# The first layer's modulation of a two-block kernel, computed by GpSimd instead of TensorE

## The chip, the cores and the metric

The kernel runs on one core of a Trainium2 chip. The metric is device time in microseconds, the median of several executions. The engines that matter are TensorE (PE in the tables, its weight loads PEld), VectorE (DVE), ScalarE (ACT), GpSimd (POOL) and SyncE (SP), which issues most loads.

## What is computed

A first block of two layers (a causal mixer, cross-attention to a memory, a gated feed-forward) works on 256 tokens of 1024 features. A second block of two layers (pooling, gating and neighbourhood attention, then a feed-forward) follows; its norms and residuals are modulated by a condition vector. The part that the change touches is this modulation, for layer 0 of the second block:

```python
silu_c  = jax.nn.silu(c)        # 1024 values, for the latents
silu_cc = jax.nn.silu(c_ctx)    # 1024 values, for the context
mod   = silu_c  @ w_mod[l] + b_mod[l]     # w_mod[l] is 1024 x 6144 float32
mod_c = silu_cc @ w_mod[l] + b_mod[l]
sh1, sc1, g1, sh2, sc2, g2 = jnp.split(mod[:, None, :], 6, axis=-1)
a = rms_norm_2(h, norm1_g[l]) * (1 + sc1) + sh1     # and so on
```

So it is a product of two rows of 1024 with a matrix of 25 MB, which depends on no activation: it can be done at any time before the second block begins.

## The kernel before

Activations are held by features: 128 partitions, eight feature tiles, 256 tokens. Every weight piece (512 KB mostly) is loaded by `pieces` through SyncE's queue into `raw` (three buffers), split by `split` into two float32r parts, `hi` by ScalarE (line 254) and `lo = raw - hi` by VectorE (line 255), four buffers each, and multiplied three times by TensorE (`mm3`, lines 226 to 228). A unit of a feed-forward of the first block (`swiglu`) takes six such pieces, and VectorE also makes the gated hidden values there (lines 779 to 783: `g` and `a` from PSUM, then `g`, `a` and the split of `a` in SBUF).

`modulation_0` is a generator of 48 steps. A step loads a 512 KB piece of `w_mod0` (four row tiles of 256 columns) through GpSimd's queue into `fraw` (three buffers), and TensorE multiplies its four row tiles by four windows of `cs`, a tile in which the two condition columns stand between columns of zeros, each on its own 32 columns of the array (line 140, a bank of PSUM `fmm`). So twelve groups of columns gather in one bank, each on its own rows. After 24 steps ScalarE copies the bank (`modrow`, line 144), two products with the selector `sel` (line 147) turn it to features and add the four quarters, and VectorE adds the bias into `modT` (line 149). The steps are placed by `tick`, which issues them behind an instruction of TensorE's (token sums, scores), and what is left is done by `modulation_done(0)` in the hook `context` of the second feed-forward. The second layer's `modulation_1` works on VectorE, later, and isn't touched.

The order of each engine's queue is made by a scheduler at build time from the program's order and its own estimates of time; on the chip each engine works through its queue in that order. An engine that waits holds up all that is queued behind.

Of the kernel before, what the change touches and what calls it, by code (L numbers as in the profile page):

```python
# [22 lines left out]
# Column offsets of the per-feature vectors (feature k * 128 + p lies at [p, offset + k]).  # L23
VEC = {}
# [16 lines left out]
def _spec():  # L41
    """How each weight matrix is cut: groups of columns in the order of use, each a list of pieces
    (first row tile, row tiles, columns) of at most 4 KB a partition."""
# [24 lines left out]
    s["w_mod0"] = cut(8, 6 * D, 256, 4)  # L68
# [30 lines left out]
class Block:  # L99
    """Weights of one stream piece, split into float32r parts whose sum they are."""  # L100
# [6 lines left out]
def kernel(ctx: ExitStack, tc: tile.TileContext, A: dict, out: bass.AP):  # L107
# [7 lines left out]
    def enter(name, side="left", **bufs):  # L115
        """Opens a pool for the temporaries with these tags (and numbers of buffers)."""
# [11 lines left out]
    def modulation_0():  # L128
        """shift, scale and gate of the first layer's streams, by features: steps of four products, for where the tensor
        engine waits. Twelve groups of 256 features share a bank, each on its rows; a quarter of the array adds up a  # L130
        quarter of the sum over the features of the condition."""
        for c in range(24):
            j = c % 12
            for off, k0, kt, n in OFFSETS["w_mod0"][c]:
                if j == 0 and k0 == 0:
                    ps = bank("fmm")
                w = temp("fraw", [128, kt, n])
                load(w.rearrange("p k n -> p (k n)"), "w_mod0", off, nc.gpsimd)
                for k in range(4):
                    nc.tensor.matmul(ps[32 * k:32 * k + 32, :256], cs[:, k0 + k, 22 - 2 * j:54 - 2 * j], w[:, k, :],  # L140
                                     start=j == 0 and k0 == 0, stop=j == 11 and k0 == 4, tile_position=(0, 32 * k))
                if j == 11 and k0 == 4:
                    m = temp("modrow", [128, 256])
                    nc.scalar.activation(m, ps[:, :256], AF.Copy)
                    ps = bank("fmm")
                    for i in range(2):
                        nc.tensor.matmul(ps[:, 32 * i:32 * i + 24], m[:, i * 128:i * 128 + 128], sel, start=True, stop=True)
                    o = VEC["b_mod_2"][0] + 2 * c - 22
                    nc.vector.tensor_tensor(modT[:, 0, 2 * c - 22:2 * c + 2, :].rearrange("p (c i) s -> p i c s", i=2),
                                            ps[:, :64].rearrange("p (i c s) -> p i c s", i=2, s=2)[:, :, :12, :],  # L150
                                            vecs[:, o:o + 24].rearrange("p (c i) -> p i c", i=2)[:, :, :, None]
                                            .to_broadcast([128, 2, 12, 2]), op=OP.add)
                yield True
# [1241 lines left out]
```

## Time and profile before

| | |
|---|---|
| median of three runs | 1993.68 us (1992.7 to 1998.14) |
| span of the profiled execution | 1991.1 us |
| PE, PEld busy | 1944.0, 1762.3 us (98%, 89%) |
| DVE, ACT, POOL busy | 1350.4, 864.3, 85.0 us |
| loads of `w_mod0` (`fraw`) | 48 of 512 KB, from GpSimd's queue |

The profiled execution's span lies 2.6 us under the median. The stages, by the first loads of their weights: the first mixer to about 135 us, its output and the first cross-attention to 200, the first feed-forward to about 390, the second layer of the first block to 590, its feed-forward to about 800, the second block from there to the end. Busy shares of an engine are averages; what is worth reading is, stage by stage, which engine has no idle time left and what it waited for. The rows have a section of their own below.

### The profile page before, as it was taken

Reading aid. Unit: us, or ns where it says so; the run is one execution under the profiler, and the core shown is the slowest. Engines: PE = TensorE matmul, PEld = TensorE weight load, DVE = VectorE, ACT = ScalarE, POOL = GpSimd, SP = SyncE. Lnnn points to the kernel's source line nnn. Section 1 sums busy time; section 2 is a strip of 40 time slices with the busy share of each in tenths; the row PEclk is TensorE's granted clock in tenths of the full one; section 3 lists DMA queues with packets and bytes.
Section 4 is the critical chain, followed back from the end, with each engine's and each line's share of the span. In section 5 each row is a group of like instructions: output and inputs, shape, how many; then the busy total and the mean of one; then the engine's idle time right before and its main releaser. Section 6 shows DMA issues by size and latency. Waiting matters only on the chain.

```text
span 1991.1 us, 34583 instructions
## 1 busy us (share of the span) xinstructions
PE 1944.0 (98%) x13852; PEld 1762.3 (89%) x13852; DVE 1350.4 (68%) x2790; ACT 864.3 (43%) x1477; POOL 85.0 (4%) x163
## 2 busy tenths in 40 slices
PE   7999999999999999999999999999999899999998
PEld 6689999998889999798788888888889898989998
DVE  7567766686686767645677765777775755667666
ACT  6565544445564444434432233333223434444444
POOL 1100000000000000000011100111100000000000
PEclk9999999999999999999999999999999999999999
DMA  7656555653356555322256532444432432554553
GB/s 262 238 182 223 180 184 182 195 184 115 120 197 223 197 180 180 100 86 67 72 163 182 164 106 85 140 151 150 151 122 86 158 106 85 185 186 142 188 184 112
DMA packets 89776, 309.43 MB, mean 155 GB/s; under 512 B 10528, under 2 KB 15552, under 8 KB 89360
## 3 DMA queue, kind: packets, MB, share of 16 engines
q1 hardware_dynamic: 74048, 254.43, 39.1%
q0 software_dynamic: 15280, 52.28, 8.1%
q8 instruction: 108, 1.77, 0.4%
q14 instruction: 52, 0.43, 0.1%
q10 hardware_dynamic: 288, 0.52, 0.1%
HBM read 306.15 MB, written 1.05 MB: 154 GB/s over the span
## 4 chain that ended last, share of the span: by engine, by line
PE 93%; issue 2%; DVE 2%; DMA 1%; ACT 1%; POOL 0%; DVEq 0%; POOLq 0%; ACTq 0%
PE mm L226 20%; PE mm L227 20%; PE mm L228 20%; PE sc L226 5%; PE sc L227 4%; PE sc L228 4%; PE pv L227 3%; PE pv L226 3%; PE pv L228 3%; PE pv L436 2%; PE sc L400 2%; PE pv L419 2%; DMA fraw<-in_w_mod 1%; PE fmm L140 1%; PE sc L358 1%
## 5 line engine op out<-in xcount | busy, mean ns | idle before, releaser
L254 ACT ACTIVATE hi<-raw 128x1024 fp32r<-128x1024 f32 (+2 forms) x466 | 487.8, 1053 | 774.0 <-PE mm L227 326.9
L255 DVE TENSOR_TENSOR lo<-raw,hi 128x1024 fp32r<-128x1024 f32 (+2 forms) x466 | 566.3, 1217 | 333.3 <-ACT hi L254 329.2
L226 PE MATMUL mm<-oph,hi 128*128 128x256 f32 (+1 forms) x1832 | 566.6, 311 | 4.2 <-ACT oph L887 2.8
L228 PE MATMUL mm<-oph,lo 128*128 128x256 f32 (+1 forms) x1832 | 567.2, 310 | 0.0
L227 PE MATMUL mm<-opl,hi 128*128 128x256 f32 (+1 forms) x1832 | 566.6, 310 | 0.0
L226 PEld LDWEIGHTS mm<-oph,hi 128*128 128x128 f32 x1832 | 350.2, 192 | 25.1 <-ACT oph L887 3.3
L228 PEld LDWEIGHTS mm<-oph,lo 128*128 128x128 f32 x1832 | 350.8, 192 | 21.7 <-issue 3.0
L227 PEld LDWEIGHTS mm<-opl,hi 128*128 128x128 f32 x1832 | 350.7, 192 | 19.0 <-issue 1.8
L226 PE MATMUL mm<-hi,oph 128*128 128x256 f32 (+1 forms) x752 | 216.9, 290 | 12.7 <-ACT hi L254 9.5
L227 PE MATMUL mm<-lo,oph 128*128 128x256 f32 (+1 forms) x752 | 217.6, 290 | 1.1 <-DVE lo L255 1.0
L228 PE MATMUL mm<-hi,opl 128*128 128x256 f32 (+1 forms) x752 | 216.6, 289 | 1.4 <-DVE opl L258 1.2
L226 PEld LDWEIGHTS mm<-hi,oph 128*128 128x128 f32 x752 | 145.4, 194 | 15.3 <-ACT hi L254 10.5
L227 PEld LDWEIGHTS mm<-lo,oph 128*128 128x128 f32 x752 | 145.4, 194 | 7.1 <-issue 3.6
L228 PEld LDWEIGHTS mm<-hi,opl 128*128 128x128 f32 x752 | 144.9, 193 | 6.0 <-issue 2.3
L227 PE MATMUL sc<-hid,hi 128*128 128x256 f32 (+1 forms) x272 | 89.0, 327 | 0.7 <-DVE hid L1193 0.7
L226 PE MATMUL sc<-hid,hi 128*128 128x256 f32 (+1 forms) x272 | 89.1, 330 | 0.0
L227 PE MATMUL pv<-hid,hi 128*128 128x256 f32 (+1 forms) x272 | 88.9, 327 | 0.0
L228 PE MATMUL sc<-hid,lo 128*128 128x256 f32 (+1 forms) x272 | 88.8, 327 | 0.0
L228 PE MATMUL pv<-hid,lo 128*128 128x256 f32 (+1 forms) x272 | 88.8, 327 | 0.0
L226 PE MATMUL pv<-hid,hi 128*128 128x256 f32 (+1 forms) x272 | 88.5, 327 | 0.0
L161 POOL DMA_DIRECT2D mraw<-in_w_mod x96 | 51.6, 538 | 600.7 <-DVE modraw L163 594.6
L163 DVE CUSTOM_DVE_ANT_0 fmm<-mraw,silu 128x512 f32<-128x512 f32 x96 | 66.7, 694 | 3.1 <-DMA mraw<-in_w_mod 3.1
(312 smaller groups left out, 3315.3 us busy)
## 6 DMA issues: line engine op xcount, KB each, us to landing
raw<-in_w_ff SPq DMA_DIRECT2D x128, 512.0 KB, 3.7
raw<-in_w_in SPq DMA_DIRECT2D x84, 512.0 KB, 3.6
fraw<-in_w_mod POOLq DMA_DIRECT2D x48, 512.0 KB, 5.4
mraw<-in_w_mod POOLq DMA_DIRECT2D x96, 256.0 KB, 3.0
raw<-in_l_w_gate SPq DMA_DIRECT2D x44, 512.0 KB, 4.2
raw<-in_l_w_up SPq DMA_DIRECT2D x44, 512.0 KB, 4.0
raw<-in_l_w_down SPq DMA_DIRECT2D x44, 512.0 KB, 4.1
raw<-in_l_w_qkv SPq DMA_DIRECT2D x24, 512.0 KB, 3.6
```

The source lines that it names most:

```text
L140: nc.tensor.matmul(ps[32 * k:32 * k + 32, :256], cs[:, k0 + k, 22 - 2 * j:54 - 2 * j], w[:, k, :], start=j == 0 and k0 == 0, stop=j == 11 ...
L161: nc.gpsimd.dma_start(out=w, in_=A["w_mod1"][c, i])
L163: nc.vector.tensor_tensor_reduce(out=w if s else bank("fmm"), in0=w, in1=silu[s][:, i * 512:i * 512 + 512], scale=1.0, scalar=0.0, op0=OP. ...
L226: nc.tensor.matmul(ps, ah, bh, start=start, stop=False, skip_group_check=shared)
L227: nc.tensor.matmul(ps, ah, bl, start=False, stop=False, skip_group_check=shared)
L228: return nc.tensor.matmul(ps, al, bh, start=False, stop=stop, skip_group_check=shared)
L254: nc.scalar.activation(hi, src, AF.Copy)
L255: nc.vector.tensor_sub(lo, src, f(hi))
L358: nc.tensor.transpose(ps[:n, j * 256 + t * 128:j * 256 + t * 128 + 128], src(t), ident)
L400: i = nc.tensor.matmul(ps, (ah, ah, al)[p], (bh, bl, bh)[p], start=p == 0, stop=p == 2)
L419: nc.tensor.transpose(ps[:, n:n + 128], P[t][:, c:c + 128], ident)
L436: nc.tensor.matmul(o[64 * h:64 * h + 64, q0:], V[kt + kk], parts[h][:, cols], start=kt + kk == 0, stop=kt + kk == total - 1, tile_position ...
```

## The change

`w_mod0` is cut into 12 groups of 512 columns, each of eight pieces of one row tile (256 KB). `modulation_0` now takes 13 steps. In a step GpSimd loads the eight row tiles one after the other (`fraw`, two buffers), multiplies each by the two per-partition condition values of that tile (`sc0`) with two `tensor_scalar`, and adds the products up in two accumulators (`macc`, three buffers, so that a step's second accumulator takes a buffer that TensorE has to have read). That is 16 multiplies and 14 adds of 128x512 float32 a step. The matmuls of the step before are written behind it: four matmuls with a column of ones (`onecol`), which only sum over the partitions, 256 columns each, on four parts of the array. After six steps ScalarE, TensorE and VectorE finish a half as before.

`tick` no longer issues steps of layer 0. One is issued before the first mixer, one within it, one ahead of the first feed-forward and nine inside it; the thirteenth (only matmuls and the end) comes with `modulation_done(0)`.

```diff
-    s["w_mod0"] = cut(8, 6 * D, 256, 4)
+    s["w_mod0"] = cut(8, 6 * D, 512, 1)
...
-                w = temp("fraw", [128, kt, n])
-                load(w.rearrange("p k n -> p (k n)"), "w_mod0", off, nc.gpsimd)
-                for k in range(4):
-                    nc.tensor.matmul(ps[32 * k:32 * k + 32, :256], cs[:, k0 + k, 22 - 2 * j:54 - 2 * j], w[:, k, :],
-                                     start=j == 0 and k0 == 0, stop=j == 11 and k0 == 4, tile_position=(0, 32 * k))
...
+        def rows_of(c, accs):
+            for s in range(2):
+                for i in range(2):
+                    r = 2 * (c % 6 * 2 + i) + s
+                    q = 32 * (2 * s + i)
+                    nc.tensor.matmul(rows_of.ps[q:q + 32, :256], onecol[:, 31 - r:63 - r],
+                                     accs[s][:, i * 256:i * 256 + 256], start=c % 6 == 0, stop=c % 6 == 5,
+                                     tile_position=(0, q))
...
+        for c in range(13):
+            accs = None
+            if c < 12:
+                accs = [temp("macc", [128, 512]) for _ in range(2)]
+                for off, k0, kt, n in OFFSETS["w_mod0"][c]:
+                    w = temp("fraw", [128, n])
+                    load(w, "w_mod0", off, nc.gpsimd)
+                    for s in range(2):
+                        p = accs[s] if k0 == 0 else w if s else temp("mprod", [128, n])
+                        nc.gpsimd.tensor_scalar(p, w, sc0[:, k0, s:s + 1], None, op0=OP.mult)
+                        if k0:
+                            nc.gpsimd.tensor_add(accs[s], accs[s], p)
+            if held is not None:
+                if held[0] % 6 == 0:
+                    rows_of.ps = bank("fmm")
+                rows_of(*held)
+            held = (c, accs)
+            yield True
...
-        if n and steps[l] is not None:
+        if n and l and steps[l] is not None:
...
-    fill, pool = enter("fill", side="right", fraw=3, modrow=1)
+    fill, pool = enter("fill", side="right", fraw=2, mprod=1, macc=3, modrow=1)
...
+        next(steps[0])
         even_mixer(m0, x0)
...
-        swiglu("l0_", f0, m1)
+        next(steps[0])
+        swiglu("l0_", f0, m1, {u: lambda: next(steps[0]) for u in range(1, 10)})
```

How the queues change, at three places. First TensorE's queue in the first cross-attention, at the token sums (`sc<-ones`; `mm<-oph,hi` and the like are the query products). Before:

```order
L328 MATMUL sc<-ones,acc 128x1
L227 MATMUL mm<-opl,hi 128x256
L228 MATMUL mm<-oph,lo 128x256
L328 MATMUL sc<-ones,sq_2103 128x1
L140 MATMUL fmm<-fraw,cs 32x256 x12
L226 MATMUL mm<-oph,hi 128x256
```

The same place in the changed kernel:

```order
L347 MATMUL sc<-ones,acc 128x1
L246 MATMUL mm<-opl,hi 128x256
L247 MATMUL mm<-oph,lo 128x256
L347 MATMUL sc<-ones,sq_2050 128x1
L245 MATMUL mm<-oph,hi 128x256
```

The three steps (twelve matmuls) behind the token sums are gone; line 140 has 192 matmuls in the whole queue before.

Second, a little further on in TensorE's queue of the changed kernel, among the scores of the cross-attention (`sc<-kx,qk`):

```order
L247 MATMUL mm<-oph,lo 128x256
L245 MATMUL sc<-kx,qk 128x256
L246 MATMUL sc<-kx,qk 128x256
L139 MATMUL fmm<-macc,onecol 32x256 x4
L247 MATMUL sc<-kx,qk 128x256
```

This is where TensorE sums up the second of the twelve steps. The queue has 48 such matmuls in 23 places, 22 of them of two matmuls and this one of four; the score products now stand behind GpSimd's sums.

Third, GpSimd's queue from the constants on. Before:

```order
L837 DMA sinks<-in_sinks 128x8
L497 DMA mask<-in_masks 128x512 x2
L208 DMA fraw<-in_w_mod 128x1024 x16
L497 DMA mask<-in_masks 128x512
L208 DMA fraw<-in_w_mod 128x1024 x32
```

In the changed kernel:

```order
L861 DMA sinks<-in_sinks 128x8
L227 DMA fraw<-in_w_mod 128x512 x2
L517 DMA mask<-in_masks 128x512 x2
L839 MEMSET onecol 128x1
L164 ISA
L164 TENSOR_SCALAR macc<-fraw,sc_83 128x512 x2
L164 TENSOR_SCALAR mprod<-fraw,sc_83 128x512
L227 DMA fraw<-in_w_mod 128x512
L166 TENSOR_TENSOR macc<-macc,mprod 128x512
L164 TENSOR_SCALAR fraw<-fraw,sc_83 128x512
```

From there on 192 multiplies, 168 adds and 96 loads alternate in one queue; the third mask's load stands behind the first step, the loads for the second layer's modulation behind the twelfth.

## Rows read from the trace of the kernel before

**Rows 1.** The page: span, busy time by engine, and the slices of the span.
```profile
span 1991.1 us, 34583 instructions
PE 1944.0 (98%) x13852; PEld 1762.3 (89%) x13852; DVE 1350.4 (68%) x2790; ACT 864.3 (43%) x1477; POOL 85.0 (4%) x163
...
POOL 1100000000000000000011100111100000000000
PEclk9999999999999999999999999999999999999999
```

**Rows 2.** Busy time by stretch: stretch in us, each engine (instructions), granted clock, DMA.
```profile
20.00:60.00 40.00, 37.11 (x320) 31.11 (x321) 35.81 (x124) 26.38 (x56) 4.22 (x8) 1.00 0.68 231
60.00:135.00 75.00, 72.15 (x548) 52.34 (x548) 47.25 (x163) 38.98 (x104) 10.32 (x20) 0.95 0.61 211
...
200.00:380.00 180.00, 179.44 (x1515) 177.98 (x1515) 117.56 (x188) 84.47 (x119) 1.57 (x3) 1.00 0.56 182
```

**Rows 3.** The same view, TensorE's line 140 alone (PE, PEld, clock, DMA).
```profile
20.00:60.00 40.00, 5.76 (x69) 1.88 (x72) 1.00 0.68 231
60.00:135.00 75.00, 14.28 (x150) 3.90 (x150) 0.95 0.61 211
135.00:200.00 65.00, 1.50 (x24) 0.68 (x24) 1.00 0.61 205
200.00:380.00 180.00, 1.50 (x24) 0.67 (x24) 1.00 0.56 182
380.00:560.00 180.00, 2.68 (x48) 1.35 (x48) 1.00 0.47 152
560.00:815.00 255.00, 7.09 (x80) 2.20 (x72) 1.00 0.56 186
```

**Rows 4.** TensorE in order of time: start, us, line, operation, [idle before, releaser].
```profile
61.23 0.64 PE L140 MATMUL fmm<-fraw,cs 128*32 128x256 f32 x8
61.80 0.39 PE L228 MATMUL mm<-oph,lo 128*128 128x256 f32 x1
...
87.69 0.95 PE L140 MATMUL fmm<-fraw,cs 128*32 128x256 f32 x8 [1.99 <-DMA fraw<-in_w_mod]
...
177.11 1.50 PE L140 MATMUL fmm<-fraw,cs 128*32 128x256 f32 x24
178.55 0.39 PE L226 MATMUL mm<-oph,hi 128*128 128x256 f32 x1
```

**Rows 5.** Busy time by stretch again, around the wait at 87.69 us.
```profile
85.00:90.00 5.00, 3.01 (x17) 1.63 (x15) 0.55 (x2) 0.88 (x2) 0.82 (x2) 0.79 0.88 338
90.00:95.00 5.00, 5.00 (x26) 4.21 (x24) 1.56 (x2) 2.67 (x4) 0.00 (x0) 0.87 0.40 127
```

**Rows 6.** GpSimd's groups: operation, shape, count, busy us, mean ns; a load's landing.
```profile
L1042 POOL MEMSET bias<- 128x512 f32 x4 | 2.0, 526 | 246.7 <-PE sc L1010 246.7
L161 POOL DMA_DIRECT2D mraw<-in_w_mod x96 | 51.6, 538 | 600.7 <-DVE modraw L163 594.6 <-DVE lo L255 6.1
...
mraw<-in_w_mod POOLq DMA_DIRECT2D x96, 256.0 KB, 3.0
```

**Rows 7.** VectorE's groups from 200 to 380 us, shapes apart.
```profile
L255 DVE TENSOR_TENSOR lo<-raw,hi 128x1024 fp32r<-128x1024 f32 x60 | 73.3, 1222 | 48.4 <-ACT hi L254 48.0
L779 DVE TENSOR_TENSOR g<-mm,rows 128x256 f32<-128x256 f32 x19 | 8.0, 423 | 4.1 <-PE mm L228 3.5 <-ACT rows L349 0.6
L783 DVE TENSOR_TENSOR a<-a,g 128x256 f32<-128x256 f32 x18 | 7.6, 425 | 0.6
L255 DVE TENSOR_TENSOR qk<-a,qk 128x256 fp32r<-128x256 f32 x18 | 7.6, 422 | 3.9 <-ACT qk L254 3.9
L782 DVE SCALAR_TENSOR_TENSOR g<-t,g 128x256 f32<-128x256 f32 x18 | 7.5, 419 | 0.0
L781 DVE TENSOR_TENSOR a<-mm,rows 128x256 f32<-128x256 f32 x18 | 7.5, 417 | 0.0
```

**Rows 8.** GpSimd and VectorE's line 477 around 111.6 us; last, line 477 undisturbed.
```profile
111.05 1.05 POOL L208 DMA_DIRECT2D fraw<-in_w_mod  x2 [8.20 <-PE fmm L140]
...
111.76 0.74 DVE L477 TENSOR_SCALAR p<-p,sm 128x128 f32<-128x128 f32 x3
...
L477 DVE TENSOR_SCALAR p<-p,sm x4: 279/346/394, 111.8 to 112.4; 128x128 f32<-128x128 f32 x2, 128x256 f32<-128x256 f32 x2
...
L477 DVE TENSOR_SCALAR p<-p,sm x4: 281/318/350, 103.4 to 104.1; 128x128 f32<-128x128 f32 x2, 128x256 f32<-128x256 f32 x2
```

**Rows 9.** TensorE at two places: the second step's sums, and the twelfth's.
```profile
181.72 0.28 PE L228 MATMUL sc<-kx,qk 128*128 128x256 f32 x1
...
810.30 0.39 PE L228 MATMUL mm<-hi,opl 128*128 128x256 f32 x1
```

More of the change, by code (lines that the diff above doesn't have):

```diff
@@ L128, in modulation_0 @@
     def modulation_0():
[L132 to L136, printed above, removed]
-                w = temp("fraw", [128, kt, n])
-                load(w.rearrange("p k n -> p (k n)"), "w_mod0", off, nc.gpsimd)
-                for k in range(4):
-                    nc.tensor.matmul(ps[32 * k:32 * k + 32, :256], cs[:, k0 + k, 22 - 2 * j:54 - 2 * j], w[:, k, :],
-                                     start=j == 0 and k0 == 0, stop=j == 11 and k0 == 4, tile_position=(0, 32 * k))
[L142 to L153, printed above, removed]
@@ new lines, in modulation_0 @@
+        held = None
+        def rows_of(c, accs):
[6 more added lines that the diff above has]
+                                     tile_position=(0, q))
+            if c % 6 == 5:
+                m = temp("modrow", [128, 256])
+                nc.scalar.activation(m, rows_of.ps[:, :256], AF.Copy)
+                ps = bank("fmm")
+                for i in range(2):
+                    nc.tensor.matmul(ps[:, 32 * i:32 * i + 24], m[:, i * 128:i * 128 + 128], sel, start=True, stop=True)
+                g = 24 * (c // 6)
+                o = VEC["b_mod_2"][0] + g
+                nc.vector.tensor_tensor(modT[:, 0, g:g + 24, :].rearrange("p (c i) s -> p i c s", i=2),
+                                        ps[:, :64].rearrange("p (i c s) -> p i c s", i=2, s=2)[:, :, :12, :],
+                                        vecs[:, o:o + 24].rearrange("p (c i) -> p i c", i=2)[:, :, :, None]
+                                        .to_broadcast([128, 2, 12, 2]), op=OP.add)
@@ L489 @@
     op2 = tuple(x[:, :, 256:512] for x in op)
-    fill, pool = enter("fill", side="right", fraw=3, modrow=1)
+    fill, pool = enter("fill", side="right", fraw=2, mprod=1, macc=3, modrow=1)
     sel = pool.tile([128, 24], F32, name="sel")
-    cs = pool.tile([128, KD, 54], F32, name="cs")
+    onecol = pool.tile([128, 63], F32, name="onecol")
+    sc0 = pool.tile([128, KD, 2], F32, name="sc0")
     b1, pool = enter("block1", v4=2, tok=2, p=4, p0=4, qk=4, pp=2)
@@ L761, in cross, with swiglu @@
                 residual(2 * j + i, ps, nxt)
-    def swiglu(l, nrm, nxt, hook=None):
+    def swiglu(l, nrm, nxt, hooks):
         act = nrm.op
@@ L797, in swiglu @@
         for u in range(9):
-            if hook is not None and u == 4:
-                hook()
+            if u in hooks:
+                hooks[u]()
             down([hidden(u)], False)
+        if 9 in hooks:
+            hooks[9]()
         down([hidden(9), hidden(10)], True)
@@ L814 @@
     nc.gpsimd.dma_start(out=sel, in_=A["sel"])
-    nc.gpsimd.memset(cs, 0.0)
+    nc.gpsimd.memset(onecol, 0.0)
+    nc.gpsimd.memset(onecol[:, 31:32], 1.0)
     cv = vecs[:, VEC["c_2"][0]:VEC["c_2"][0] + 16].rearrange("p (s k) -> p k s", s=2)
@@ L819 @@
     nc.vector.tensor_scalar(sg, sg, 0.5, 0.5, op0=OP.mult, op1=OP.add)
-    nc.vector.tensor_mul(cs[:, :, 22:24], sg, cv)
+    nc.vector.tensor_mul(sc0, sg, cv)
     m0 = Normed("l0_mix_norm")
@@ L911, in block1 @@
         cross("l0_", x0, f0, keys1)
-        swiglu("l0_", f0, m1)
+        next(steps[0])
+        swiglu("l0_", f0, m1, {u: lambda: next(steps[0]) for u in range(1, 10)})
         odd_mixer(m1, x1)
@@ L917, in block1 @@
         ffn, _ = enter("ffn", qk=4)
-        swiglu("l1_", f1, fin, context)
+        swiglu("l1_", f1, fin, {4: context})
         ffn.close()
```

## The prediction

> **What bounds the kernel now.** I read the page's busy shares first, then busy time by stretch, then the groups of the engines that the change loads. TensorE is busy 98% of the span, with the granted clock at its upper level nearly throughout; GpSimd is busy 4%, all of it issuing loads and writing constants [rows 1]. By stretch, the first feed-forward (200 to 380 us) leaves TensorE 0.6 us idle in 180, so there the time is TensorE's, and VectorE, which feeds it, works 117.6 of the 180 us. The first mixer is another matter: from 20 to 60 us VectorE has 35.8 of 40, from 60 to 135 us TensorE has 72.2 of 75, but part of that is the modulation itself [rows 2]. So two questions decide: what TensorE gains when 144 of its 192 modulation matmuls go, and what VectorE loses when GpSimd, so far nearly idle, computes beside it for some 800 us.
>
> **What TensorE gets back.** Line 140 takes 20.0 us before 135 us and 12.8 us after [rows 3]. One step costs 0.57 us from its start to the next matmul's, three together 1.44 [rows 4]: 0.43 us a step and 0.14 for opening. A place of the new kernel holds two matmuls (once four) of the same 256 columns. A pair alone is a form that I can bound by the half and the whole of a step (0.29 to 0.57); I take 0.57, since its columns stream as long as a step's. 23 places then cost 13.1 us, two of them (1.1) before 135 us and 21 (12.0) behind. The products with the selector are as before.
> - Behind 135 us: 12.8 - 12.0 = 0.8 us, in stretches where TensorE has no idle time, so the whole of it is gained; 1.
> - Before 135 us: 20.0 - 1.1 = 18.9 us. One wait for a piece of `w_mod0` goes too, 2.0 us at 87.69 [rows 4], and the ten microseconds behind it had a granted clock of 0.79 and 0.87 [rows 5], worth 5 x 0.21 + 5 x 0.13 = 1.7 us. At most 22.6. At least 0: these steps were put where TensorE would have waited. The 5.8 us of them between 20 and 60 us I count as nothing, since VectorE is 90% busy there; of the other 14.3 - 1.1 + 3.7 = 16.9 I take three quarters, because VectorE has only 47 of 75 us to do there [rows 2]; 13.
> Together a gain of 14 us, between 1 and 23.5.
>
> **What GpSimd has to do.** A step is 16 multiplies, 14 adds and eight loads. No compute instruction of GpSimd's stands in the trace. The nearest is its MEMSET of the same 128x512 float32, one stream, 0.53 us [rows 6]. If a multiply's read and write lie on each other it takes that, if they follow each other 1.05; an add, with a second operand, 0.53 to 1.58. I take the middles, 0.79 and 1.05, a mean of 0.91 us, because nothing is nearer to one end. The loads cost 8 x 0.54 = 4.3 us to issue [rows 6], and as the queue runs (load, add, load, then the multiply that needs the first load) GpSimd waits for a landing four times a step, 3.0 - 1.05 - 0.54 = 1.4 us each [rows 6], 5.6 together. Undisturbed, a step takes 27.3 + 4.3 + 5.6 = 37 us.
> How much time it has follows from TensorE's queue: counting the weight matmuls ahead of the second and the twelfth step's sums, the kernel before reached these places at 181.7 and 810.3 us [rows 9], 62.9 us a step. TensorE would wait for GpSimd only where an instruction, with its own waits, took over (62.9 - 4.3 - 5.6) / 30 = 1.77 us. Alone, GpSimd is in time.
> The Trainium skill, GPSIMD Engine Reference, § 3.1, has 4497 ns for an add of 2048 float32 and 769 ns for 512 elements of a one-input loop; an estimate from that page is 0.93 us for the mean instruction here, and with it the sum below would rise by 9 us. No row here shows it.
>
> **What it costs VectorE.** Two instructions of VectorE's in the trace show that GpSimd can hold it up. A `p` of 128x128 on line 477 takes 281 ns; the first of those that start at 111.76 us took 394, while GpSimd issued loads from 111.05 to 112.10, and it ended at 112.15, just behind [rows 8]. The subtractions of line 255 were not stretched by loads (1222 ns on average [rows 7]), but GpSimd has not yet read a tensor beside them. So a VectorE instruction with two tensors from SBUF may wait for nothing, or for the whole GpSimd instruction under way: 0 to 0.91 us each. I take the whole, by the one kind of wait that rows 8 shows, which lasts to the other's end.
> The Trainium skill, SBUF — State Buffer, § Who interferes with whom, says the same against this change: a VectorE instruction with two SBUF inputs and a GpSimd instruction that reads SBUF exclude each other for a whole instruction, with no sharing. By that rule the times below hold; without it the first rival's does. Rows 8 agrees for one form, and no run here shows it for two inputs.
> In the first feed-forward a unit takes 18 us (60 subtractions in 180 us, six a unit), VectorE 11.8 of it [rows 2, 7]. Of these, (60 + 18 + 18 + 18) / 10 = 11.4 instructions read two tensors from SBUF; `g` and `a` from PSUM (1.6 us) read one and can run beside GpSimd [rows 7]. Taking turns, a unit costs VectorE 11.8 + 11.4 x 0.91 - 1.6 = 20.6 us: 2.6 over TensorE's 18. GpSimd's 30 instructions last 30 / 11.4 = 2.63 units, 54 us, in which TensorE loses 6.8 us. In the other 8.7 us of a step VectorE's idle third (6.2 of 18) catches up 3.0. A step costs 3.8 us, the ten steps from 181.7 us on 38.
> In the first mixer the first step falls on the stretch where VectorE is idle 4.2 of 40 us [rows 2]: at 1.77 us each some 20 GpSimd instructions there cost 20 x 0.91 - 4.2 = 14 us if all count, 0 if the chains there wait for something else; 10. The second step I count at nothing: VectorE has 28 of 75 us idle there [rows 2], which hides 30 x 0.91 = 27 us; without that cover it would cost as the others do, 4 us.
> The new loads are as many bytes as before, spread to 810 us, where DMA has half its time free [rows 2]; nothing. The masks' load stands behind two loads, 1 us later than before and long before the scores; nothing. The third mask waits for the first step and the second layer's loads for the twelfth: both are needed far behind; nothing, unless GpSimd is late.
>
> **The sum.** 1991.1 - 14 + 38 + 10 = 2025.1 us of span, and 2.6 for what lies between this execution and the median: 2027.7; **2028 us**, 1.7% slower.
>
> **The rivals.**
> *GpSimd works beside VectorE* without holding it up, or its instructions are as short as 0.53 us (11.8 + 6.0 - 1.6 = 16.2 us a unit, under 18): then only TensorE's gain is left, 1991.1 - 14 + 2.6 = 1980, with 1970 to 1992 as its ends; **faster**. For it: the subtractions beside loads keep their 1.22 us. Against: rows 8.
> *GpSimd comes too late.* VectorE's waits are GpSimd's as well: if each of its instructions has to let a subtraction of 1.22 us pass, it takes 2.13 us, over the 1.77 from which TensorE waits. A step is then 30 x 2.13 + 9.9 = 73.8 us, 10.9 over 62.9; ten steps 109: 1991.1 - 14 + 109 + 10 + 2.6 = 2099. TensorE's queue stands at the sums, with the weight products behind them.
> *It cancels.* VectorE's cushion of four `lo` buffers, three subtractions ahead, or chains that never needed the removed steps, bring gain and loss within 6 us: 1988 to 2000.
>
> **How the numbers follow.** A measurement of this kernel can tell about 0.3% (6 us) from no change. Taking turns, 2028, has a chance of 0.50, with 2000 to 2088 as its own range (the upper end is a mean GpSimd instruction of 1.03 us: 11.8 + 11.7 - 1.6 = 21.9 us a unit, 10.3 us a step less 1.8, ten steps 85, and a gain of TensorE's of only 1; at the lower end GpSimd's waits fall on VectorE's idle time twice as often, 19 instead of 38, and the first mixer loses nothing); beside each other, 1980, 0.26; cancelled 0.12; too late, 2099, 0.12. Faster by over 0.3% is 0.27 (the first rival and a little of the third), within 0.3% 0.11, slower 0.62. The range runs from 1976, leaving out the lower third of the first rival, to 2090, leaving out most of the last.
>
> **What would show it.** Subtractions of line 255's form well over 1.22 us while GpSimd computes, and `hi` or `lo` as the releaser of TensorE's waits in the feed-forward, would show the turns; unchanged subtractions there and a span near 1978 the first rival. Waits of TensorE's at the sums of `macc`, released by GpSimd, would show the second. GpSimd's mean of 0.91 us is read from its groups. The gain before 135 us shows in when the output product of the first mixer begins. The forecast is wrong if VectorE's waits stay within its idle third, or if GpSimd needs far less or more than 0.91 us.

## The result and the profile after

The changed kernel takes 2063.34 us (median of 4, 2056.75 to 2068.91) against 1993.81: a ratio of 1.0345, with a 95% interval of 1.032 to 1.0369. It is slower, as forecast, inside the range, but by 70 us where the forecast had 34. The profiled execution has a span of 2067.1 us. The page's lines that answer to [rows 1]:

```profile
span 2067.1 us, 34428 instructions
PE 1964.1 (95%) x13564; PEld 1783.1 (86%) x13564; DVE 1502.2 (73%) x2790; ACT 868.5 (42%) x1477; POOL 728.6 (35%) x572
...
POOL 8584886787877778810002110010010000000000
PEclk8999999999998999999999999999999999999999
```

VectorE has the same 2790 instructions and is busy 152 us longer; TensorE has 288 fewer and is busy 20 us longer. By stretch, as [rows 2]:

```profile
20.00:60.00 40.00, 26.13 (x162) 24.88 (x162) 39.95 (x86) 14.54 (x25) 38.23 (x27) 0.72 0.37 117
60.00:135.00 75.00, 67.01 (x456) 56.31 (x457) 60.35 (x181) 44.21 (x118) 49.11 (x37) 0.92 0.37 124
200.00:380.00 180.00, 164.02 (x1271) 157.70 (x1271) 133.69 (x172) 74.69 (x111) 140.88 (x97) 0.95 0.52 173
380.00:560.00 180.00, 172.13 (x1339) 156.83 (x1337) 148.25 (x270) 83.07 (x151) 144.59 (x97) 0.98 0.50 171
560.00:815.00 255.00, 235.49 (x1826) 223.88 (x1825) 203.12 (x309) 116.88 (x196) 197.64 (x135) 0.96 0.52 176
```

From 200 to 380 us TensorE now idles 16 us, at a granted clock of 0.95, although VectorE has 46 us to spare: the bound has not moved to VectorE, TensorE waits for single results. GpSimd's groups (line 164 multiplies, 166 adds), which [rows 6] had to stand in for:

```profile
L164 POOL TENSOR_SCALAR fraw<-fraw,sc 128x512 f32<-128x512 f32 x84 | 174.3, 2075 | 0.0
L164 POOL TENSOR_SCALAR mprod<-fraw,sc 128x512 f32<-128x512 f32 x84 | 151.7, 1806 | 70.5 <-DMA fraw<-in_w_mod 70.0
L166 POOL TENSOR_TENSOR macc<-macc,mprod 128x512 f32<-128x512 f32 x84 | 130.1, 1549 | 3.6
L166 POOL TENSOR_TENSOR macc<-macc,fraw 128x512 f32<-128x512 f32 x84 | 122.0, 1452 | 1.5
...
L164 POOL TENSOR_SCALAR macc<-fraw,sc 128x512 f32<-128x512 f32 x24 | 43.9, 1832 | 103.2 <-PE fmm L139 95.8 <-DMA fraw<-in_w_mod 7.3
```

The shortest tenth of the multiplies took 1.56 us and of the adds 1.28, 1.43 on average; the forecast had 0.91. GpSimd still waited 96 us for TensorE to read its accumulators, and no wait of TensorE's was released by it: it was not late. VectorE's groups from 200 to 380 us, beside [rows 7]:

```profile
L274 DVE TENSOR_TENSOR lo<-raw,hi 128x1024 fp32r<-128x1024 f32 x51 | 74.6, 1465 | 33.0 <-ACT hi L273 32.9
L803 DVE SCALAR_TENSOR_TENSOR g<-t,g 128x256 f32<-128x256 f32 x14 | 11.5, 821 | 0.0
L274 DVE TENSOR_TENSOR qk<-a,qk 128x256 fp32r<-128x256 f32 x14 | 10.6, 758 | 2.4 <-ACT qk L273 2.4
...
L800 DVE TENSOR_TENSOR g<-mm,rows 128x256 f32<-128x256 f32 x15 | 6.3, 417 | 2.5 <-PE mm L247 1.7 <-ACT rows L368 0.8
L802 DVE TENSOR_TENSOR a<-mm,rows 128x256 f32<-128x256 f32 x15 | 6.2, 412 | 0.0
```

What reads two tensors from SBUF got longer (1.22 to 1.47 us, 0.42 to 0.82 and 0.76); what reads one operand from PSUM kept its 0.42. Scalar forms, which read one tensor from SBUF, got longer too and make some 30 of the 162 us of the table of stages below: `p` of the first block's attention in the kernel before (line 477) and in the changed one (line 496).

```profile
L477 DVE TENSOR_SCALAR p<-p,sm 128x256 f32<-128x256 f32 x32 | 9.8, 349 | 0.0
L477 DVE TENSOR_SCALAR p<-p,sm 128x128 f32<-128x128 f32 x32 | 7.7, 291 | 0.4
L496 DVE TENSOR_SCALAR p<-p,sm 128x256 f32<-128x256 f32 x32 | 16.1, 542 | 0.0
L496 DVE TENSOR_SCALAR p<-p,sm 128x128 f32<-128x128 f32 x32 | 14.8, 516 | 0.2
```

So there are turns. How they look, GpSimd (POOL) and VectorE in order of time, start and length first:

```profile
283.21 1.29 POOL L166 TENSOR_TENSOR macc<-macc,mprod 128x512 f32<-128x512 f32 x1
284.48 2.79 POOL L164 TENSOR_SCALAR fraw<-fraw,sc 128x512 f32<-128x512 f32 x1
```

```profile
283.41 2.17 DVE L274 TENSOR_TENSOR lo<-raw,hi 128x1024 fp32r<-128x1024 f32 x1 [0.26 <-ACT hi L273]
285.50 0.41 DVE L803 SCALAR_TENSOR_TENSOR g<-t,g 128x256 f32<-128x256 f32 x1
285.95 0.72 DVE L804 TENSOR_TENSOR a<-a,g 128x256 f32<-128x256 f32 x1
```

The subtraction that begins within the add ends 1.08 us after it: with 1.22 us of its own, it waited for nearly all of the add. The multiply behind is beside that subtraction and two more instructions, and there it is the multiply that takes longer, 2.79 for 1.56, while `a` loses 0.3.

And what it does to TensorE, in the output products ahead of the first feed-forward:

```profile
229.42 2.04 POOL L166 TENSOR_TENSOR macc<-macc,fraw 128x512 f32<-128x512 f32 x1
231.41 1.48 POOL L166 TENSOR_TENSOR macc<-macc,mprod 128x512 f32<-128x512 f32 x1
```

```profile
230.23 1.50 DVE L277 SCALAR_TENSOR_TENSOR opl<-xT,vecs,oph 128x256 fp32r<-128x256 f32 x1
231.66 0.41 DVE L585 TENSOR_TENSOR xT<-mm,xT 128x256 f32<-128x256 f32 x1
231.99 1.45 DVE L328 TENSOR_TENSOR acc<-acc,sq 128x512 f32<-128x512 f32 x1
233.37 1.21 DVE L274 TENSOR_TENSOR lo<-raw,hi 128x1024 fp32r<-128x1024 f32 x1
234.50 1.22 DVE L277 SCALAR_TENSOR_TENSOR opl<-xT,vecs,oph 128x256 fp32r<-128x256 f32 x2
```

```profile
235.38 0.56 PE L246 MATMUL mm<-opl,hi 128*128 128x256 f32 x1 [2.37 <-DVE opl L277]
235.73 0.41 PE L247 MATMUL mm<-oph,lo 128*128 128x256 f32 x1
235.95 0.41 PE L245 MATMUL mm<-oph,hi 128*128 128x256 f32 x1
...
239.87 0.28 PE L246 MATMUL mm<-opl,hi 128*128 128x256 f32 x1
239.99 0.28 PE L247 MATMUL mm<-oph,lo 128*128 128x256 f32 x1
```

Two operands `opl` and a sum of squares are held up one after the other, and TensorE stands still 2.37 us. Then its products follow 0.21 us apart until 238.7, and only from there 0.12 again: the lower of the two clock levels, for 16 products, costs 1.5 us more. Over the whole way from the 800th to the 5600th weight product (184 to 847 us before) TensorE needs 662.7 us before and 734.9 after; it idles 8.6 and 50.5 of them, so 42 us are waits and 30 us slower work; 295 products follow 0.21 us behind the one before where 111 did, which is 184 x 0.094 = 17 us of the 30.

### The profile page after: what moved, and what is told of

It reads as the page before. It is cut to its first block, busy times and chain, and to the rows that moved or that the text cites. A ratio compares the mean times of both kernels' runs of the same rounds, so it can differ in the third digit from the quotient of the medians.

```text
span 2067.1 us, 34428 instructions
## 1 busy us (share of the span) xinstructions
PE 1964.1 (95%) x13564; PEld 1783.1 (86%) x13564; DVE 1502.2 (73%) x2790; ACT 868.5 (42%) x1477; POOL 728.6 (35%) x572
## 3 DMA queue, kind: packets, MB, share of 16 engines
q1 hardware_dynamic: 74048, 254.43, 35.8%
HBM read 306.15 MB, written 1.05 MB: 149 GB/s over the span
## 4 chain that ended last, share of the span: by engine, by line
PE 79%; DVE 12%; ACT 2%; issue 2%; DMA 1%; DVEq 0%; ACTq 0%
PE mm L246 17%; PE mm L245 17%; PE mm L247 17%; DVE lo L274 4%; PE sc L245 4%; PE sc L246 4%; PE sc L247 4%; PE pv L246 3%; PE pv L245 3%; PE pv L247 3%; PE pv L455 2%; PE sc L419 2%; PE pv L438 2%; ACT hi L273 1%; DVE g L803 1%
## 5 line engine op out<-in xcount | busy, mean ns | idle before, releaser
L274 DVE TENSOR_TENSOR lo<-raw,hi 128x1024 fp32r<-128x1024 f32 (+2 forms) x466 | 607.7, 1306 | 278.6 <-ACT hi L273 274.7
L246 PEld LDWEIGHTS mm<-opl,hi 128*128 128x128 f32 x1832 | 355.0, 194 | 25.8 <-DVE opl L277 6.4
L164 POOL TENSOR_SCALAR mprod<-fraw,sc 128x512 f32<-128x512 f32 x84 | 151.7, 1806 | 70.5 <-DMA fraw<-in_w_mod 70.0
L164 POOL TENSOR_SCALAR fraw<-fraw,sc 128x512 f32<-128x512 f32 x84 | 174.3, 2075 | 0.0
L166 POOL TENSOR_TENSOR macc<-macc,mprod 128x512 f32<-128x512 f32 x84 | 130.1, 1549 | 3.6
L166 POOL TENSOR_TENSOR macc<-macc,fraw 128x512 f32<-128x512 f32 x84 | 122.0, 1452 | 1.5
L246 PE MATMUL pv<-hid,hi 128*128 128x256 f32 (+1 forms) x272 | 88.9, 327 | 0.0
```

What stands on the lines that cost most here:

```text
L164: nc.gpsimd.tensor_scalar(p, w, sc0[:, k0, s:s + 1], None, op0=OP.mult)
L166: nc.gpsimd.tensor_add(accs[s], accs[s], p)
L246: nc.tensor.matmul(ps, ah, bl, start=False, stop=False, skip_group_check=shared)
L274: nc.vector.tensor_sub(lo, src, f(hi))
```

## The experiments

Times are medians; "none" is the kernel without the first layer's modulation, 1972.7 us. The line numbers of rows differ a little from kernel to kernel, and the names are the same.

**What is there to win and to lose.** First, GpSimd's arithmetic left out: it only loads, and TensorE sums two raw row tiles.

```diff
-                    for s in range(2): ... tensor_scalar, tensor_add
+                    accs.append(w)        # TensorE sums accs[-2:]
```

> GpSimd only loads the 96 row tiles; its 192 multiplies and 168 adds are left out, and TensorE sums the last two row tiles of each step as they are, in the same 48 matmuls (so the modulation's values are others). Turns of VectorE and GpSimd: all of the loss goes and TensorE's gain is left, 1980 us (1970 to 1992), subtractions of line 274's form back at 1.22 us. Rival, the new order of TensorE's queue and a lower granted clock without the fills make the loss: it stays, 2040 us or more.

Measured: 1979.63 us (0.993, 0.9908 to 0.9952). Without the arithmetic the loss is gone and 14 us are gained, the number that the forecast had for TensorE; the arithmetic, with the places that the sums take because of it, costs 2063.3 - 1979.6 = 84 us. TensorE's queue is not the same in the two kernels: with nothing to wait for, the scheduler put all 48 sums ahead of 194 us, in 15 places, where the changed kernel has them in 23 places up to 891 us. Next, the kernel before without its steps (no loads of `w_mod0`, the bias alone as modulation):

```diff
-        for c in range(24): ...               # loads, matmuls, ends of the halves
+        nc.vector.tensor_copy(modT[:, 0], vecs[:, o:o + 48, None].to_broadcast([128, 48, 2]))
```

> The kernel before without the first layer's modulation: no loads of its weights, no matmuls, the bias alone in modT. What it can give back at most: 32.8 us of TensorE's busy time if all of it was on the path, 14 us by the forecast's working (13 of 22.6 in the first mixer, and here 12.8 more behind it): 1991 - 13 - 12.8 + 2.6 = 1968 us (1958 to 1980).

Measured: 1972.71 us (0.9896, 0.9878 to 0.9914). All of the modulation was worth only 22 us to begin with; that is what any way of computing it could win, but for the few microseconds that another order of the queues brings. Then one of the two conditions only, 8 multiplies and 7 adds a step:

```diff
-                    for s in range(2): ...
+                    p = accs[0] if k0 == 0 else w
+                    nc.gpsimd.tensor_scalar(p, w, sc0[:, k0, 0:1], None, op0=OP.mult)
+                    if k0: nc.gpsimd.tensor_add(accs[0], accs[0], p)
```

> GpSimd multiplies by one of the two conditions only: 8 multiplies and 7 adds a step, half its arithmetic, and TensorE sums that accumulator twice (the second condition is left out). Turns, paid by GpSimd's time: half of the loss, 1980 + 42 = 2022 us (2008 to 2035). Rival, a loss from VectorE lacking cushion only once both engines are nearly full: much less than half, under 2000 us.

Measured: 2005.49 us (1.0069, 1.0042 to 1.0095). Half of the instructions cost 26 of the 84 us, less than half: between my 2022 and the rival's "under 2000".

**Which instruction holds VectorE up.** Multiplies alone, adds alone, and one and a half times the multiplies (GpSimd as long at work as in the changed kernel):

```diff
 multiplies alone (with one and a half times as many: s in (0, 0, 1))
+                    for s in range(2):
+                        nc.gpsimd.tensor_scalar((accs[0], w)[s], w, sc0[:, k0, s:s + 1], None, op0=OP.mult)
 adds alone (w0: the first row tile)
+                    for s in range(2):
+                        if k0: nc.gpsimd.tensor_add(accs[s], w0 if k0 == 1 else accs[s], w)
```

> The adds are left out; the 16 multiplies of a step stay, and TensorE sums the last two products. 16 x 1.56 = 25 us of GpSimd a step against 8 x 1.56 + 7 x 1.28 = 21.4 with one condition (2005) and 43 in the changed kernel (2063). If the loss goes by GpSimd's reading time, between these two, about 2015 (2005 to 2030). Rival: adds, which read two tensors, do the damage; then under 1990.

> The multiplies are left out; the 14 adds of a step stay (of raw row tiles). 14 x 1.28 = 18 us of GpSimd a step. By GpSimd's reading time: a little under the kernel with one condition, about 2000 (1990 to 2005). Rival, that adds do the damage: 2030 and above.

> No adds; 24 multiplies a step (each row tile's first product is made twice), 24 x 1.83 = 44 us of GpSimd a step, as much as in the changed kernel (43 undisturbed). If GpSimd's time counts, 2063. If multiplies hold VectorE up only a little and adds do the damage, one and a half times the 20 us that 16 multiplies cost: 2010 (2000 to 2025).

Measured: 1999.91 (1.0027, 1.0011 to 1.0043), 2086.97 (1.0467, 1.0445 to 1.0489) and 2008.51 (1.0082, 1.0055 to 1.0109). GpSimd's time does not decide: 359 us of busy time, with adds, cost 107 over the kernel without arithmetic, 645 us, with multiplies, 29. My "by reading time" failed for the adds, where the rival was right; the 16 multiplies came between the two (2005 to 2030, or under 1990). `lo` from 200 to 815 us, with multiplies alone and with adds alone:

```profile
L272 DVE TENSOR_TENSOR lo<-raw,hi 128x1024 fp32r<-128x1024 f32 x180 | 223.5, 1243 | 117.2 <-ACT hi L271 116.3
```

```profile
L273 DVE TENSOR_TENSOR lo<-raw,hi 128x1024 fp32r<-128x1024 f32 x164 | 237.7, 1453 | 75.2 <-ACT hi L272 74.4
```

The trace of the changed kernel says the same, sorted by what GpSimd was doing when a subtraction began: 49 began within an add that had 0.78 us left on average and got 0.65 longer; 103 began within a multiply that had 0.96 left and got 0.04 longer. Short instructions (`g`, `a`, `opl`, `qk`) lose 0.9 to 1.1 us behind an add, 0.0 to 0.3 behind a multiply. The scalar form `p`, which reads one tensor, is held up like them: 0.74 us longer where it began within an add (11 cases, 0.93 us left), 0.22 within a multiply (42 cases, 0.98 left). So an add, which reads two tensors, keeps out what reads SBUF on VectorE almost until it ends; a multiply, which reads one, hardly does, and takes longer itself (2.05 us beside such instructions, 1.62 without, 137 and 55 cases). That the number of tensors read makes the difference is my reading; the runs show it for these two instructions. Adds alone cost more than adds among multiplies, and not because VectorE is held up longer in all: some 148 us against 162, by the account of the table of stages below. Two adds now follow each other directly and single hold-ups are longer (1.2 us on average against 0.6), and GpSimd, quicker without multiplies, does more of its work early: 84 of the 148 us fall into the first mixer and the start of the first feed-forward, where 73 us are lost for them, against 47 of the 162 in the changed kernel. Which of the two weighs more no run separates. With adds alone, GpSimd and VectorE at 230 us, where one subtraction, begun 0.45 us ahead of the first add, ends 1.09 us behind the second:

```profile
230.68 2.52 POOL L164 TENSOR_TENSOR macc<-macc,fraw 128x512 f32<-128x512 f32 x2
```

```profile
230.23 4.06 DVE L273 TENSOR_TENSOR lo<-raw,hi 128x1024 fp32r<-128x1024 f32 x1
```

Every instruction cut in two:

```diff
+                        for h in (slice(0, 256), slice(256, 512)):
+                            nc.gpsimd.tensor_scalar(p[:, h], w[:, h], sc0[:, k0, s:s + 1], None, op0=OP.mult)
+                        ...                              # and the adds
```

> Every GpSimd instruction is cut into two of 256 columns (32 multiplies and 28 adds a step), nothing else. In the changed kernel an undisturbed multiply took 1.56 us and an add 1.28. If what counts is how long one GpSimd instruction holds VectorE up, the halves (estimates: 0.8 and 0.65 us) halve the loss of 84 us over the kernel without GpSimd arithmetic: 1980 + 42 = 2022. If what counts is GpSimd's time in all, or if a fixed part of each instruction eats what is saved, about 2063 or more; over 2080 would mean that VectorE now gives way twice as often.

Measured: 2070.46 (1.0384, 1.0362 to 1.0407). Halves take 0.91 and 0.72 us undisturbed where half of the whole instruction's time is 0.78 and 0.64, GpSimd's own time grows, and TensorE now does wait for it at the sums, 21 us in five places. VectorE is lengthened by 123 us instead of 162, and what that saves goes to those waits. The whole computation with ScalarE multiplying:

```diff
-                        nc.gpsimd.tensor_scalar(p, w, sc0[:, k0, s:s + 1], None, op0=OP.mult)
+                        nc.scalar.activation(p, w, AF.Copy, scale=sc0[:, k0, s:s + 1])
```

> The whole modulation, but the 16 multiplies of a step are made by ScalarE (a copy scaled by the per-partition condition); GpSimd only adds. GpSimd as in the kernel with adds alone, so about 2000 if ScalarE's 16 x 0.55 = 9 us a step (an estimate from its 1.05 us for a `hi` of 1024 columns) fit into its idle time (95 of 180 us in the first feed-forward before the change). Rival: the scaled copies delay the `hi` parts that VectorE and TensorE wait for, 2015 to 2030. Either way slower than the kernel before (1994) by this theory, and faster than the changed one.

Measured: 2076.65 (1.042, 1.0401 to 1.0438): near adds alone, and slower than the changed kernel, which the expectation had ruled out. The cause is open: VectorE is held up less than with adds alone (107 against 148 us), and ScalarE's copies took 0.72 us each where I had 0.55, 138 us in all, so the late `hi` parts of the rival may have their share.

**Writes.** Three constant writes, or one, in place of each multiply and add:

```diff
-                        nc.gpsimd.tensor_scalar(p, ...)          # and tensor_add(accs[s], ...)
+                        for _ in range(3): nc.gpsimd.memset(p, 0.5)   # and accs[s]; or once
```

> Each of GpSimd's 360 instructions is replaced by three memsets of the same 128x512 tile, about as long together (3 x 0.53 us against 1.56 and 1.28), which write and read nothing; the products and sums are left out. Turns that arise only where GpSimd reads: two-input instructions of VectorE's keep their times, and the kernel takes as long as without GpSimd's arithmetic, 1980 us (1972 to 1995), with waits only where tensor_scalar of 128x256 is stretched. Rival, any work of GpSimd's holds VectorE up: 2050 us or more, subtractions at 1.4 us.

> Every multiply and add is replaced by one constant write of the same tile (30 a step, 0.5 us each; three of them each gave 2211). By that run's trace writes hold up only VectorE's scalar, copy and reciprocal-root forms, and these until the queue of writes has a pause; two-input subtractions stay at 1.22 us. A row tile's writes now take 4 x 0.47 = 1.9 us with a wait for a load behind them, so these forms wait some 2 us and not 20 to 37: 1980 to 2010. If writes hold up whatever they meet: 2040 or more.

Measured: 2211.17 (1.1088, 1.1014 to 1.1162) and 2003.65 (1.0058, 1.0035 to 1.008). The first was expected at 1980; the second lies inside its range. VectorE's groups of the first, from 20 to 815 us:

```profile
L276 DVE TENSOR_TENSOR lo<-raw,hi 128x1024 fp32r<-128x1024 f32 x156 | 195.8, 1258 | 81.6 <-ACT hi L275 80.6
L498 DVE TENSOR_SCALAR p<-p,sm 128x128 f32<-128x128 f32 x32 | 60.7, 3628 | 0.2
L288 DVE TENSOR_SCALAR sm<-sm 128x2 f32<-128x2 f32 x6 | 35.9, 5980 | 0.1
```

Subtractions are left alone by writes, but scalar forms (0.29 us for `p` of 128x128 in the kernel before, 0.17 for `sm`) wait through long stretches of GpSimd's stream of writes. One lasts 19 us beside writes that follow each other every 0.47 us and last 0.54, so that none ends before the next has begun:

```profile
39.54 19.32 DVE L285 TENSOR_SCALAR sm<-sm 128x2 int32<-128x2 int32 x1
```

```profile
57.80 0.54 POOL L165 MEMSET mprod<- 128x512 f32 x1
58.28 0.54 POOL L229 DMA_DIRECT2D fraw<-in_w_mod  x1
58.80 0.54 POOL L168 MEMSET macc<- 128x512 f32 x1
```

It ends at 58.86, just behind a load that GpSimd issues among its writes, as most of the long ones do; but three loads had gone by before (at 40.83, 46.96 and 53.09) without ending it, and no run shows what sets the fourth apart. With single writes a load comes behind every few of them, and 63 us of lengthening are left, 56 of them before 185 us.

**What a microsecond of VectorE costs.** VectorE alone makes the modulation (0.74 us for a fused multiply and add, 132 us in all), GpSimd only loads; or GpSimd multiplies and VectorE adds:

```diff
-                        nc.gpsimd.tensor_scalar(...); nc.gpsimd.tensor_add(accs[s], accs[s], p)
+                        nc.vector.tensor_add(accs[s], accs[s], p)        # the adds only, or
+                        nc.vector.scalar_tensor_tensor(out=accs[s], in0=w, scalar=sc0[:, k0, s:s + 1], in1=accs[s], op0=OP.mult, op1=OP.add)
```

> The whole modulation, but VectorE makes it (16 instructions a step, a multiply or a fused multiply and add of 128x512); GpSimd only loads. From 0.48 us for the fused form at 256 columns and 0.42 against 0.69 for 256 and 512 columns of an add, an estimate of 0.75 us each, 12 us a step, 140 us in all: as much as GpSimd lengthened VectorE's instructions in the changed kernel (136 us), with no other engine in the way. If VectorE's idle third covers added time, as the forecast had it (22 us a step), 1980. If time added to VectorE is paid for because it makes single links of the chains to TensorE late, between 2000 and 2060; if the price is as in the changed kernel, 2060.

> The whole modulation: GpSimd multiplies as in the changed kernel, VectorE adds (14 x 0.69 = 9.6 us a step, 115 in all). Multiplies alone cost 20 us (2000 against 1980). If adds on GpSimd are what holds VectorE up, and VectorE's own adds find idle time, about 2000 to 2010; if VectorE's time is paid for as it comes, 2040 or more.

Measured: 2064.07 (1.0354, 1.0334 to 1.0375) and 2052.2 (1.0301, 1.0258 to 1.0344). No instruction of VectorE's is held up in the first, and yet it costs as much as the change; the second, too, came out where added time is paid for. The added instructions of the first had all fallen before 290 us, nearly half into the first mixer:

```profile
60.00:135.00 75.00, 53.48 (x286) 41.98 (x285) 68.30 (x183) 26.25 (x72) 16.40 (x30) 0.70 0.51 153
```

So I compared by stage, between the same weight products (those of `mm3`, counted in order) in each trace: the time lost against "none", less 0.6 us for each place of sums (0.56 in the trace) and each half's end, divided by the time by which VectorE got longer (held up, or with added instructions):

| stage (weight products) | changed kernel | VectorE alone | GpSimd multiplies, VectorE adds |
|---|---|---|---|
| first mixer (0 to 300) | 16.2 / 25.7 = 0.63 | 44.6 / 63.0 = 0.71 | 12.8 / 22.6 = 0.57 |
| its output, cross-attention (to 780) | 2.9 / 7.9 = 0.37 | 13.1 / 43.2 = 0.30 | 5.6 / 13.2 = 0.42 |
| end of it, first feed-forward's start (to 1400) | 17.4 / 21.8 = 0.80 | 25.8 / 30.1 = 0.86 | 18.2 / 26.9 = 0.68 |
| first feed-forward (to 2400) | 8.7 / 17.8 = 0.49 | none left | 13.6 / 33.8 = 0.40 |
| second layer's mixer, cross-attention (to 3600) | 12.2 / 35.8 = 0.34 | | 17.6 / 49.7 = 0.35 |
| second feed-forward's start (to 3800) | 10.6 / 11.4 = 0.93 | | 1.7 / 7.5 = 0.23 |
| second feed-forward (to 5600) | 15.1 / 41.6 = 0.36 | | |

I call the quotient the price of a microsecond. But for one short stage it is much the same in these three kernels, whatever made VectorE longer: 0.6 to 0.9 in the first mixer and where a feed-forward begins, 0.3 to 0.5 elsewhere. Over all it is 83 / 162 = 0.51 in the changed kernel. The stage doesn't set it alone, though. By the same account half the arithmetic paid 23 / 77 = 0.29 in all (0.5, 0, 0.5, 0.3 and 0.3 in the first five stages) and adds alone 107 / 148 = 0.72 (0.9, 0.7, 0.9, 0.4, 0.7): with half as many hold-ups a microsecond was cheaper, with hold-ups twice as long it was dearer.

For the steady feed-forward I then put known amounts of VectorE time there, without GpSimd, as parts of the modulation: three steps (35.5 us) one pair of instructions behind every second subtraction, or in three clusters; two steps (23.7 us) within the chain of the gated values, between `g` and `a`, or behind every third subtraction; and these last two with every queue but for the pairs in the order that the scheduler makes without them.

```diff
+                    with tc.issue_after(i.ins):      # i: the subtraction, or the instruction `g`
+                        next(steps[0], None)         # two fused instructions of VectorE's
+    for queue: tc.add_manual_dep(each instruction, the one ahead of it in the order without pairs)   # fixed order
```

> Only three of the twelve steps are computed (the rest of the first layer's modulation is left out), by VectorE alone: 24 pairs of fused multiply-adds, one pair behind every second subtraction of the first feed-forward, so 24 x 2 x 0.74 = 35.5 us spread evenly over some 145 us. Base: no modulation at all, 1973, and 1 for four places of sums. The forecast's premise, that VectorE's idle third covers what is added to it (118 + 36 of 180 us), gives 1974. If added VectorE time is paid for at the price that the changed kernel showed (69 us lost for 128 us by which VectorE's instructions were longer, 0.54), 1974 + 19 = 1993.

> The same three steps on VectorE, but begun at three places of the first feed-forward, so that the 16 instructions of a step stand close together (one or two behind each VectorE instruction). By VectorE's total 1974 again. If it is the density that makes the chains late, 12 us of VectorE added in about 18 us each time, with 11.8 of 18 taken already, leaves 5.7 us a step too much: 1974 + 3 x 5.7 = 1991, and more than with the even spread.

> Two of the twelve steps on VectorE (the rest of the first layer's modulation is left out): 16 pairs of fused multiply-adds, 1.48 us a pair, 23.7 us in all, each pair between `g` and `a` of a gated value in the first feed-forward, so within a chain that TensorE waits for. If it matters where VectorE's time falls, TensorE now pays most of it, and for the clock as well: 1973 + 15 to 30 = 1988 to 2003. If only VectorE's total counts, as behind the subtractions: 1973 + 0.2 x 24 = 1978.

> The same 16 pairs, each behind a subtraction of a weight piece (every third) instead, where three more subtractions are ahead of need. By the three even steps (7.5 us for 35.5): 1973 + 5 = 1978; by the price that the changed kernel showed, 0.54, 1986.

> The 16 pairs of the kernel with pairs in the chain (1970), behind the same instructions `g`, but every engine's queue keeps the order that the scheduler makes for a kernel without any pair: the lengthening of VectorE, 23.7 us, is now unknown to the scheduler, as GpSimd's hold-ups are in the changed kernel. No sums (1 us less); the other steps of the first layer's modulation are left out as there. If time that the scheduler didn't plan for is what costs: at the 0.6 to 1.0 us of loss per us of lengthening of the first feed-forward's traces, 1972 + 14 to 24 = 1986 to 1996. If not: 1970 to 1973 again.

> The 16 pairs behind every third subtraction (1980 in the scheduler's own order), every engine's queue in the order made without them. If the order without knowledge of the pairs costs: above 1980, 1986 to 1996. If the place (in front of the next subtraction) is what costs: 1980 as before.

| kernel | us | ratio to before | over none |
|---|---|---|---|
| three steps, even | 1980.25 | 0.9937 (0.9918 to 0.9956) | 7.5 |
| three steps, clusters | 1976.16 | 0.9916 (0.9898 to 0.9935) | 3.5 |
| two steps in the chain | 1969.65 | 0.988 (0.9865 to 0.9895) | -3.1 |
| two steps behind subtractions | 1979.87 | 0.9928 (0.9911 to 0.9944) | 7.2 |
| in the chain, fixed order | 1971.78 | 0.989 (0.9874 to 0.9907) | -0.9 |
| behind subtractions, fixed order | 1977.89 | 0.9918 (0.9904 to 0.9933) | 5.2 |

A tenth to a third of the added time is lost, none of it in the chain. These differences are a little too low, since up to 780 products, ahead of all pairs, the kernels are up to 3.5 us faster than "none" by another order. By the account of the stages, from 780 to 2400 in the profiled executions, the prices are 0.26 (even), 0.13 (clusters), 0.47 and 0.24 (behind subtractions, own and fixed order), and 0.01 and 0.05 in the chain. Three of my explanations fall here: bursts (clusters cost less than the even spread), the chain of the gated values (free), and an order made without knowledge of the delay (no dearer). A few microseconds here are also what a different order alone brings. In the steady feed-forward VectorE's idle third covers half or more of what is put there in regular pieces, and all of it in the chain. Why GpSimd's hold-ups cost 0.49 in that stage, and VectorE's adds behind GpSimd's products 0.40, at the upper end of that, is not settled: they come irregularly and several in a row, as at 230 us above, but no run separates that.

## Why the forecast was half right

**TensorE's gain, 14 us: too large,** though the kernel without arithmetic gains just that, with its sums in other places. The price of 0.57 us for a pair of sums was right: the trace has 0.56 for a place of two or four. Ahead of the 780th product (181.5 us) the steps of the kernel before cost 16 us over "none", and the new sums 1: a gain of 15, near the forecast. Behind it the steps cost only 5 us, not the 11.3 for which they were busy there [rows 3], and the new sums and the ends of the halves 14 (23 x 0.6): a loss of 9 where the forecast had the two about equal. Together 6 us are gained, 8 less than forecast; why the late steps cost so little no run shows.

**Turns: right in kind.** Rows 8 showed the right sort of wait, and its scalar form is held up by adds as the two-tensor forms are. The Trainium skill, SBUF — State Buffer, § Who interferes with whom, which the forecast put beside it, agrees with the adds, with the operands from PSUM that kept their 0.42 us, and with the writes that left subtractions alone; for multiplies the traces differ (0.04 us longer with 0.96 left), and they decide.

**GpSimd's instruction, 0.91 us: wrong**, 1.43, the multiply at the upper end and beyond (1.56 where the bounds were 0.53 and 1.05): one constant write was too far from it. It had little effect, since GpSimd kept up.

**The wait of 0.91 us at each of VectorE's two-tensor instructions: too large.** The forecast gave VectorE 30 x 0.91 = 27.3 us a step, 273 in ten. From 185 us on 201 of its 871 instructions were lengthened, by 0.64 us each: 128 us, 12.8 a step. An instruction meets GpSimd only sometimes, waits only for the rest of what is under way, and behind a multiply for almost nothing.

**The idle third that pays for it: the step that failed.** The sum lets a unit's VectorE time grow until it passes TensorE's, and charges only the excess: 38 of 273 us, a price of 0.14. From the 780th product on the change lost 78 us against "none", 14 of them for 21 places of sums and the ends of two halves, so 64 of 128: a price of 0.50. The premise failed in the steady feed-forwards that it was read from (23.8 of 59 us lost, 0.40) and more so outside them, where the busy shares of one steady stage had been carried: more than half of those 128 us lie in attention, mixers and the starts of the feed-forwards, at 0.58 on average and up to 0.9. TensorE doesn't wait for VectorE's total but for single results, as at 235 us above, and a wait takes the granted clock down with it, which the sum had only for the one place in [rows 5].

The size of the waits and their price erred against each other, and that 2028 came as near as it did is luck. With the waiting alone mended the sum's own rule would charge nothing: a step of 30 x 1.43 + 9.9 = 53 us lasts 2.9 units, so a unit of VectorE's grows to 11.8 + 12.8 / 2.9 = 16.2 us, under TensorE's 18, and the forecast would have been 1991.1 - 14 + 10 + 2.6 = 1990, no loss at all. With the price alone mended (273 x 0.5 = 137) it would have been 2127. Term by term the forecast had -14 + 38 + 10 us; the profiled execution has -6 + 64 + 19, 77 where its span is 76 us longer.

**The first mixer, 10 us for the first step and none for the second: too small**, 19 us by the same account (20.3 up to the 780th product, less two places of sums). There [rows 2] had shown VectorE with 4 of 40 us idle; the first step met it there, at a price of 0.63.

**The rivals.** GpSimd beside VectorE gives 1980: the kernel without arithmetic is at 1979.6, so its number came out, with the sums in other places, and its condition is false; with multiplies alone it nearly holds (2000). GpSimd too late: not in the changed kernel, where it waited for TensorE; cutting its instructions brought the first such waits. Cancelled: no.

None of the kernels that compute everything beats the one before (2052 to 2077 against 1994); the ceiling is 22 us.

## What to carry to other kernels

An idle engine is not free when a busy one reads SBUF beside it: look at which instructions meet; here multiplies on GpSimd cost 20 us and adds of two tensors, in less of its time, 107. Price a delay stage by stage, by what waits next for the delayed instruction, and not by an engine's idle share; in a steady stream with operands ahead that share paid for half or more of regular additions, at the seams between stages for little. Before moving work off the busiest engine, leave it out once: that shows what the move can bring at most.

## What the runs showed of the hardware

- A GpSimd multiply of 128x512 float32 by a per-partition value takes 1.56 us, an add of two such tensors 1.28; halves of 256 columns 0.91 and 0.72.
- An add of GpSimd's holds up a VectorE instruction with two SBUF tensors nearly to its end (0.65 us for 0.78 left), a scalar form with one too (0.74 for 0.93), two adds in direct succession to the end of the second (4.06 us for a subtraction of 1.22); a multiply adds 0.04 us to a subtraction and up to 0.3 to a short one.
- Constant writes of GpSimd's in close succession hold up VectorE's scalar forms, 19 us in the row above, up to one of the loads issued among them, and leave two-tensor subtractions alone (1.26 us).
